# A two-block layer kernel on one core: gate steps as a pipeline, small products in one tile shape, other buffers and queues in the expert passes

## The chip, the cores and the metric

The kernel runs on one core of one Trainium2 chip. The metric is the device time of one execution in microseconds (us). A core has TensorE (PE, with its weight loads shown apart as PEld), VectorE (DVE), ScalarE (ACT), GpSimd (POOL) and SyncE (SP), and 16 DMA engines that serve the queues on which SP and ACT issue transfers.

## The reference

Two blocks are computed for 256 tokens of width 2048, all in fp32. The first has a recurrent time mix, an attention and an expert layer, the second a state-space scan and a windowed attention. The expert layer is the part on which most of the change bears: every token picks 16 of 16,384 experts in each of 8 heads, from the products of 128 by 128 keys.

```python
def step(S, inp):                       # recurrent mix, per head of 64
    r_t, k_t, v_t, kk_t, a_t, w_t = inp
    sa = jnp.einsum('bhvk,bhk->bhv', S, -kk_t)
    S = (S * w_t[:, :, None, :] + sa[..., None] * (kk_t * a_t)[:, :, None, :]
         + v_t[..., None] * k_t[:, :, None, :])
    return S, jnp.einsum('bhvk,bhk->bhv', S, r_t)
...
eid = jnp.take_along_axis(cand_id, pos, axis=-1)
gate = jax.nn.softmax(top_s, axis=-1).astype(h.dtype)
...
act = jax.nn.gelu(jnp.einsum('nd,nhkd->nhk', hx, expert_u[e]), approximate=False)
return jnp.einsum('nhk,nhkd->nd', gt * act, expert_v[e])
...
y_diag = jnp.einsum("bgcqs,bgrcqs,bcsgrp->bcqgrp", cb, decay_in, x_c)     # the scan
y_off = jnp.einsum("bcqgn,bcgrpn,bgrcq->bcqgrp", c_c, start_states, jnp.exp(da_cum))
return (y_diag + y_off).reshape(bsz, seqlen, nh, hp)
```

## The kernel before, in words

Large products run on PE as three: weights and tokens are split into a high part in the reduced fp32r form and a low rest, and hi times hi, hi times lo and lo times hi are added. `K.split` (L138 to L142) makes a split: ACT writes `hi`, then DVE or POOL subtracts it for `lo`. `K.wload` (L144) brings a weight tile of 1 MB from memory on SP's queue into one of two `raw` buffers. PE's line for a hi product has 512 columns, that for a lo product 256.

The stages, in us from the span's start: norm, the input product and the attention to 235; the recurrent mix, whose pairs of heads are woven with the input product, to 705; gates, output product and the expert query to about 1009; the first expert pass to 1862; the second to 2590; then the second block, with the scan groups inside 2650 to 3065.

**Pairs of heads** (`pair`, L442 to L688). Beside the split products they use small plain fp32 products, each of which is two records in the trace. `psA` (L464 to L467) has one of 64 rows of contraction, one of 128 and one of 32; `psS` (L547 to L558) 64 rows, head by head; `psQ` (L643) fills 64 of the 128 output columns of the array; `psY` (L659 to L666) mixes products of 64 and of 128 output columns. A row `64*128` in the trace gives rows and columns of such a tile.

**First expert pass** (`Peer.up`, L1159). All 16,384 experts are multiplied with all tokens, 128 of them (called "an expert" below) per step of the loop, with 1 MB of `peer_u`. The tile is turned on DVE (`tr`, L1172, four buffers), split in two halves c = 0 and c = 1 (L1176, `hi` and `lo` with three buffers each), and each half feeds eight hi and eight lo products (L1191, L1192). After both halves ACT copies a half of the sum (L239), DVE adds (L241), ACT applies the activation (L1200), and after every fourth expert ACT issues a store (L1202).

**Gates** (`Peer.gates`, L1118). The gate of every expert and token is the product of two one-hot factors. A step handles four tokens: DVE makes `oh2`, DVE or ACT the weighted `oh1` (two ACT instructions a token at L1145 and L1146), PE multiplies four 128 by 128 matrices into `psg` (L1151), and ACT copies `psg` to `scr` (L1132) in the next step. Every eighth step stores 2 MB to memory. There are 64 steps, 32 for each half of the tokens; the loop in `peer` (L1309 to L1317) spreads them over the first pass by a plan of rates (`UP_PLAN`, `G = 32`), one step per expert towards its end.

**Second expert pass** (`Peer.down`, L1219). For every eight experts (`B = 8`) ACT issues one load of 1 MB of activations and one of 1 MB of gates into two slots (L1240, L1241); DVE multiplies them (L1247), ACT and POOL split, and PE multiplies with `peer_v` (L1232 to L1234).

**Scan groups** (`Mamba.group`, L1465 to L1536). For two heads `psy` takes four products with 64 output columns (L1524) and two of full shape (L1526, L1529).

The order of instructions on each engine is set by a scheduler that simulates the program; buffers and an explicit tie (`issue_after`) bound it.

Of the kernel before, what the change touches and what calls it, by code (L numbers as in the profile page):

```python
# [9 lines left out]
F32 = mybir.dt.float32  # L10
F32R = mybir.dt.float32r
# [3 lines left out]
AF = mybir.ActivationFunctionType  # L15
ALU = mybir.AluOpType
# [4 lines left out]
T = 256  # L21
# [3 lines left out]
DMA_K = 2  # L25
# [85 lines left out]
class K:  # L111
# [32 lines left out]
    def wload(self, src, n=512):  # L144

        nc = self.nc
        raw = self.wp.tile([128, 4, 512], F32, tag="raw", bufs=RAW_BUFS, name="raw")
        if len(src.shape) == 3:
            for k in range(0, 4, DMA_K):
                nc.sync.dma_start(raw[:, k:k + DMA_K, :n], src[:, k:k + DMA_K])  # L150
        else:
            for c in range(4):
                nc.sync.dma_start(raw[32 * c:32 * c + 32, :, :n], src[c])
        return raw
# [219 lines left out]
class Rwkv:  # L374
# [56 lines left out]
    def lora(self):  # L431
        k, nc, pool = self.k, self.k.nc, self.pool
        th = self.th = pool.tile([65, T], F32, name="th")
        nc.vector.memset(th[64:65, :], 1.0)
        nc.scalar.activation(th[0:64, :], self.z[24][0:64, :], AF.Tanh)
        self.za = self.z[24]
        for z in (self.z[25], self.z[26][0:32]):
            k.sigmoid(z, z)

    WIDTH = 3  # L440

    def pair(self, hp):  # L442
# [15 lines left out]
        nc.scalar.dma_start(wg[:, 0, :], k.a["w_gate_up"][0, 0:128, fs])  # L458
        nc.scalar.dma_start(wg[0:32, 1, :], k.a["w_gate_up"][0, 128:160, fs])
# [87 lines left out]
        for h in range(2):  # L547
            ps = k.bank("psS").rearrange("p (a c b t) -> p a c b t", a=2, c=2, b=2)
            for tt in range(2):
                for cc in range(2):  # L550
                    E.matmul(ps[:, tt, cc], lhsT=two(BK[halves[h], tt, 2 * cc:2 * cc + 2]),
                             rhs=AR[halves[h], :, tt, halves[cc]], start=True, stop=True)
            for i, hs in enumerate(halves):
# [82 lines left out]
        for tt in range(2):  # L636
            starts = []
            for cc in range(2):
                cs = halves[cc]
                starts.append(Sd)  # L640
                if Sd is not None:
                    ps = k.bank("psQ")
                    E.matmul(ps[cs, 0:128], lhsT=At[:, tt, cs], rhs=Sd, start=True, stop=True)  # L643
# [15 lines left out]
            psY = k.bank("psY")  # L659
            for cc, s in enumerate(starts):  # L660
                cs = halves[cc]
# [326 lines left out]
class Peer:  # L988
# [129 lines left out]
    def gates(self, tt, scr, g_d, act):  # L1118
# [6 lines left out]
        late = None  # L1125
# [3 lines left out]
        def store(t0, ps):  # L1129
            c, t = divmod(t0, n)  # L1130
            st = scr[:, c % 2]
            S.copy(st.rearrange("p (i t) -> p i t", t=n)[:, :, t:t + 4], ps.rearrange("p (t i) -> p i t", t=4))  # L1132
            if t == n - 4:
                S.dma_start(g_d[c], st)

        for t0 in range(128 * tt, 128 * tt + 128, 4):
            ps = k.bank("psg")
            o2 = self.pool.tile([128, 4, 128], F32, tag="oh2", bufs=2, name="oh2")
            nc.vector.tensor_tensor(o2, key, tok(i2, t0), op=ALU.is_equal)
            o1 = self.pool.tile([128, 4, 128], F32, tag="oh1", bufs=2, name="oh1")  # L1140
            for j in range(4):
# [5 lines left out]
                else:  # L1147
                    nc.vector.tensor_scalar(o1[:, j], self.iota, i1[:, t:t + 1], w[:, t:t + 1], op0=ALU.is_equal,  # L1148
                                            op1=ALU.mult)
            for j in range(4):  # L1150
                nc.tensor.matmul(ps[:, j * 128:(j + 1) * 128], lhsT=o2[:, j], rhs=o1[:, j], start=True,  # L1151
                                             stop=True)
            if late:
                store(*late)
            late = (t0, ps)
            yield
        store(*late)

    def up(self, act_d):  # L1159
# [16 lines left out]
        def split(n, c):  # L1176
            hi, lo = (k.wp.tile([128, 8, 128], F32R, tag=n, bufs=HL_BUFS, name=n) for n in ("hi", "lo"))
# [41 lines left out]
    def down(self, scr, act_d, g_d, h, finish):  # L1219
# [6 lines left out]
        B = 8  # L1226
        held = []
# [7 lines left out]

        for i in range(128):
            raw = k.wload(V[i * 128:i * 128 + 128, :].rearrange("p (k f) -> p k f", k=4))
            if i % B == 0:
                x, g = (scr[:, 2 * (i // B % 2) + u, :].rearrange("p (i t) -> p i t", t=T) for u in range(2))
                nc.scalar.dma_start(x, act_d[:, i:i + B])  # L1240
                nc.scalar.dma_start(g.rearrange("p i t -> p (i t)").rearrange("p (c f) -> p c f", c=T // n),  # L1241
                                    g_d[:, :, i * n:(i + B) * n].rearrange("c p f -> p c f"))
                gv = g.rearrange("p i t -> p (i t)").rearrange("p (c i t) -> p c i t", c=T // n, i=B)
            if i % 2 == 0:
                xi = x[:, i % B:i % B + 2]
                xv = xi.rearrange("p i (c t) -> p c i t", t=n)
                nc.vector.tensor_tensor(xv, xv, gv[:, :, i % B:i % B + 2], op=ALU.mult)  # L1247
# [43 lines left out]
def peer(k, x2, xq, norm, hh, h_d, g_d, act_d, acts, es, finish):  # L1291
# [11 lines left out]
    with tc.tile_pool(name="up", bufs=1) as up:  # L1303
        pe.pool = up
        main = pe.up(act_d)
        route = [pe.route(up, tt) for tt in range(2)]
        gates = [pe.gates(tt, two, g_d, act) for tt, act in enumerate(GATE_ACT)]
        side = pe.anchored(itertools.chain(route[0], alternate(route[1], gates[0]), gates[1]))
        R, G, due = pe.ROUTE_STEPS, 32, 0.0  # L1309
# [61 lines left out]
class Mamba:  # L1371
# [93 lines left out]
    def group(self, g):  # L1465
# [36 lines left out]
        for hh in range(0, 8, 4):  # L1502
            M = []
            for ch in range(2):
# [12 lines left out]
                yield  # L1517
            for u in range(2):
                j = (hh + 2 * u) // 2
                hA = hh + 2 * u  # L1520
                ps = k.bank("psy")
                for ch in range(2):
                    for e in range(2):
                        E.matmul(ps[64 * e:64 * e + 64, ch * 128:(ch + 1) * 128], lhsT=xd[:, ch, hA + e, :],  # L1524
                                 rhs=M[ch][:, 2 * u + e, :], start=True, stop=True)
                E.matmul(ps[:, 256:384], lhsT=st[:, hA * 64:hA * 64 + 128], rhs=C[:, 128:256], start=True, stop=True)  # L1526
                db = W("db", [128, 2, 64])
                P.tensor_copy(db, self.dar[:, 1, h0 + hA:h0 + hA + 2, None].to_broadcast([128, 2, 64]))
                E.matmul(ps[:, 384:512], lhsT=db.rearrange("p e d -> p (e d)"), rhs=c["le"], start=True, stop=True)  # L1529
                ec = W("ec", [128, 128])  # L1530
                S.activation(ec, ps[:, 384:512], AF.Exp)
                V.tensor_tensor(ec, ps[:, 256:384], ec, op=ALU.mult)
                x = xs[j]
                V.scalar_tensor_tensor(x, x, self.dcol[:, 4 * g + j:4 * g + j + 1], ps[:, 0:T], op0=ALU.mult, op1=ALU.add)
# [525 lines left out]
```

## Time and profile before

| | |
|---|---|
| median of 3 runs | 3730.88 us (3727.95 to 3734.87) |
| the profiled execution's own time | 3734.22 us |
| its span | 3732.4 us |
| mean granted TensorE clock | 0.992 of full speed |
| busy over the span | PE 96%, PEld 80%, DVE 71%, ACT 53%, POOL 36% |
| mean DMA rate | 183 GB/s, 681.22 MB in all |

The profile is of one execution. PE's busy time is modelled: matmuls overlap, so the start of the next record is what tells how long one takes. A stage is read by the engines' busy time in its stretch, then by the waits there, each given with the instruction that ended it. In the view by stage a row gives the stretch, its length, then for PE, PEld, DVE, ACT and POOL the busy time with the number of instructions in brackets, the mean granted clock of PE as a share of full speed, the busy share of the DMA engines and GB/s.

### The profile page before, as it was taken

What the parts mean: (1) busy time and instruction counts of PE and PEld (TensorE: products, weight loads), DVE (VectorE), ACT (ScalarE), POOL (GpSimd) and SP (SyncE); (2) the same over time, 40 slices, a digit from 0 to 9 for tenths busy, and PEclk for the clock granted to TensorE, in tenths of its full rate; (3) what the DMA queues carried; (4) which work ended last, traced back from release to release, by engine and by line L of the source; (5) the groups of instructions that cost most, each with busy time, mean ns of one, the idle gap of its engine ahead of it and who ended that gap; (6) DMA issues with size and microseconds to landing.
All of it is one profiled execution on the core that took longest, in us unless ns stands there. A gap on an engine that the chain in (4) does not pass through costs nothing.

```text
span 3732.4 us, 56118 instructions
## 1 busy us (share of the span) xinstructions
PE 3596.9 (96%) x19815; PEld 2991.2 (80%) x19815; DVE 2663.3 (71%) x4261; ACT 1990.3 (53%) x3745; POOL 1329.2 (36%) x1328
## 2 busy tenths in 40 slices
PE   9999999999999999999899999999999999989998
PEld 7678888878888888877788888888788887878777
DVE  5766777667598898888644544446988879667776
ACT  5455555545454777666444444445555656445553
POOL 1333123221278777655511111111234444242101
PEclk9999999999999999999999999999999999999999
DMA  7443333467698888878877677665554445645444
GB/s 221 137 156 127 117 122 128 149 223 248 173 203 208 197 211 219 209 179 205 217 245 237 235 236 239 225 197 187 168 169 147 139 134 167 193 148 178 145 127 136
DMA packets 358334, 681.22 MB, mean 183 GB/s; under 512 B 43981, under 2 KB 111477, under 8 KB 354853
## 3 DMA queue, kind: packets, MB, share of 16 engines
q1 hardware_dynamic: 305216, 591.50, 54.3%
q10 hardware_dynamic: 52837, 86.14, 6.9%
q8 instruction: 157, 2.57, 0.3%
q14 instruction: 124, 1.02, 0.1%
HBM read 627.57 MB, written 47.22 MB: 181 GB/s over the span
## 4 chain that ended last, share of the span: by engine, by line
PE 45%; DVE 8%; issue 2%; ACT 1%; DMA 1%; POOL 0%; ACTq 0%; DVEq 0%; POOLq 0%
PE g L205 12%; PE g L207 6%; PE gv L1234 5%; PE gv L1233 5%; PE gv L1232 5%; DVE tr L1172 2%; DVE lo L142 2%; PE dv L1233 2%; PE dv L1232 2%; PE dv L1234 2%; DVE oh L1148 1%; ACT hi L140 1%; PE g L229 1%; PE g L230 1%; PE g L228 1%
## 5 line engine op out<-in xcount | busy, mean ns | idle before, releaser
L142 DVE TENSOR_TENSOR lo<-raw,hi 128x1024 fp32r<-128x1024 f32 (+3 forms) x856 | 1045.6, 1224 | 671.7 <-ACT hi L140 662.2
L140 ACT CAST hi<-raw 128x1024 fp32r<-128x1024 f32 (+3 forms) x858 | 868.2, 1015 | 957.5 <-PE g L205 336.4
L205 PE MATMUL g<-x,hi 128*128 128x512 f32 x3040 | 1089.0, 400 | 13.6 <-DVE x L1642 9.3
L207 PE MATMUL g<-x,lo 128*128 128x256 f32 x3040 | 843.5, 288 | 12.0 <-DVE lo L142 11.4
L1191 PE MATMUL gu<-x,hi 128*128 128x512 f32 x2048 | 734.1, 398 | 4.2 <-ACT hi L140 4.0
L142 POOL TENSOR_TENSOR lo<-tr,hi 128x512 fp32r<-128x512 f32 x429 | 593.0, 1411 | 265.7 <-ACT hi L140 184.6
L205 PEld LDWEIGHTS g<-x,hi 128*128 128x128 f32 x3040 | 567.5, 189 | 133.9 <-issue 18.3
L207 PEld LDWEIGHTS g<-x,lo 128*128 128x128 f32 x3040 | 574.0, 189 | 47.7 <-DVE lo L142 21.7
L1192 PE MATMUL gu<-x,lo 128*128 128x256 f32 x2048 | 581.7, 284 | 16.8 <-POOL lo L142 11.5
L1191 PEld LDWEIGHTS gu<-x,hi 128*128 128x128 f32 x2048 | 387.2, 189 | 91.9 <-ACT hi L140 6.0
L1192 PEld LDWEIGHTS gu<-x,lo 128*128 128x128 f32 x2048 | 388.0, 189 | 25.3 <-POOL lo L142 19.5
L1172 DVE STREAM_TRANSPOSE tr<-raw 128x1024 f32<-128x1024 f32 x256 | 309.4, 1232 | 87.1 <-POOL lo L142 47.1
L140 ACT CAST hi<-tr 128x512 fp32r<-128x512 f32 x512 | 289.9, 617 | 68.9 <-PE gu L1191 39.4
L142 POOL TENSOR_TENSOR g<-scr,g 128x512 fp32r<-128x512 f32 x64 | 112.3, 1756 | 574.3 <-ACT g L140 574.3
L1234 PE MATMUL gv<-hi,g 128*128 128x512 f32 x756 | 299.7, 396 | 0.0
L1233 PE MATMUL gv<-lo,g 128*128 128x512 f32 x756 | 299.7, 396 | 0.0
L1232 PE MATMUL gv<-hi,g 128*128 128x512 f32 x756 | 238.4, 396 | 0.0
L1200 ACT ACTIVATE act<-act 128x256 f32<-128x256 f32 x128 | 53.6, 419 | 239.3 <-DVE act L241 221.9
L205 PE MATMUL g<-y2m,hi 128*128 128x512 f32 x512 | 173.5, 395 | 0.0
L1233 PEld LDWEIGHTS gv<-lo,g 128*128 128x128 f32 x756 | 142.4, 188 | 34.7
L1234 PEld LDWEIGHTS gv<-hi,g 128*128 128x128 f32 x756 | 142.4, 188 | 34.7
L1232 PEld LDWEIGHTS gv<-hi,g 128*128 128x128 f32 x756 | 142.4, 188 | 34.7
(601 smaller groups left out, 5871.0 us busy)
## 6 DMA issues: line engine op xcount, KB each, us to landing
raw<-in_peer_u_dram SPq DMA_DIRECT2D x512, 256.0 KB
raw<-in_peer_v_dram SPq DMA_DIRECT2D x256, 512.0 KB
raw<-in_a_w_in_dram SPq DMA_DIRECT2D x160, 512.0 KB
raw<-in_w_in_dram SPq DMA_DIRECT2D x136, 512.0 KB
raw<-in_b_w_in_dram SPq DMA_DIRECT2D x64, 512.0 KB
raw<-in_a_w_out_dram SPq DMA_DIRECT2D x48, 512.0 KB
raw<-in_w_out_dram SPq DMA_DIRECT2D x32, 512.0 KB
raw<-in_w_peer_query_dram SPq DMA_DIRECT2D x32, 512.0 KB
```

The lines of the kernel that those rows point to most:

```text
L140: ins = nc.scalar.copy(hi, x) if heng == "act" else nc.vector.tensor_copy(hi, x)
L142: return ins, eng.tensor_tensor(lo, x, hi.bitcast(F32), op=ALU.subtract)
L205: nc.tensor.matmul(ps[f], lhsT=hi[:, k, f * 128:(f + 1) * 128], rhs=x2[:, q, :], start=(q == 0), stop=False)
L207: nc.tensor.matmul(ps[f][:, 0:T], lhsT=lo[:, k, f * 128:(f + 1) * 128], rhs=x2[:, q, 0:T], start=False, stop=(q == nk - 1))
L228: nc.tensor.matmul(ps[tt], lhsT=x, rhs=w, start=(q == 0), stop=False)
L1172: st["t"] = nc.vector.transpose(tr.rearrange("p b (u j) -> p u b j", u=2), raw[:, 2 * u:2 * u + 2].rearrange("p u (b j) -> p u b j", j=32))
L1191: nc.tensor.matmul(ps, lhsT=hi[:, j], rhs=self.hn2[:, q, :], start=(q == 0), stop=False)
L1192: st["m"] = nc.tensor.matmul(ps[:, 0:T], lhsT=lo[:, j], rhs=self.hn2[:, q, 0:T], start=False, stop=(q == KT - 1))
L1200: nc.scalar.activation(o, o, AF.Gelu)
L1232: nc.tensor.matmul(p, lhsT=x, rhs=hi, start=first, stop=False)
L1233: nc.tensor.matmul(p, lhsT=x, rhs=lo, start=False, stop=False)
L1234: nc.tensor.matmul(p, lhsT=g2[:, T + tt * 128:T + tt * 128 + 128], rhs=hi, start=False, stop=last)
```

## The change

1. *Gates.* A step now stores the product made one step ago, issues the product of the factors made one step ago, and makes factors for the next. The factors lie in a part of `hh` that is free then, three deep, not in tiles of their own. Each half has 34 steps for 32, and the plan's `G` is 34.
2. *First pass.* Halves c = 1 go to tiles of their own, `hi1` and `lo1` with two buffers, beside the three for c = 0.
3. *Second pass.* Loads are of 512 KB for four experts, on SP, in four slots; each is tied behind the weight fetch issued last, and the load of the next four experts is issued one expert into the present four.
4. *Small products.* `psA` and `psQ` use the full 128 by 128 shape over rows that are zero (memsets in `lora` and for `wg`); `psS` alternates between the two row halves; `psY` makes both heads at once and two copies take what is wanted; the scan's full-shape products come before the small ones of both units.

```diff
-                nc.sync.dma_start(raw[:, k:k + DMA_K, :n], src[:, k:k + DMA_K])
+                self.fetch = nc.sync.dma_start(raw[:, k:k + DMA_K, :n], src[:, k:k + DMA_K])
...
+        nc.gpsimd.memset(self.z[24][0:64], 0.0)
+        for r in (slice(32, 64), slice(64, 128)):
+            nc.gpsimd.memset(self.z[26][r], 0.0)
...
+        P.memset(wg[32:64, 1, :], 0.0)
...
-        E.matmul(psA[:, 0:T], lhsT=wg[64:128, 1, :], rhs=self.za[64:128, :], start=True, stop=True)
+        E.matmul(psA[:, 0:T], lhsT=wg[:, 1, :], rhs=self.z[24], start=True, stop=True)
         E.matmul(psA[:, T:], lhsT=wg[:, 0, :], rhs=self.z[25], start=True, stop=False)
-        E.matmul(psA[:, T:], lhsT=wg[0:32, 1, :], rhs=self.z[26][0:32, :], start=False, stop=True)
+        E.matmul(psA[:, T:], lhsT=wg[:, 1, :], rhs=self.z[26], start=False, stop=True)
...
+        for tt in range(2):
+            for cc in range(2):
+                for h in range(2):
+                    E.matmul(both[h][:, tt, cc], lhsT=two(BK[halves[h], tt, 2 * cc:2 * cc + 2]),
                              rhs=AR[halves[h], :, tt, halves[cc]], start=True, stop=True)
...
-                    E.matmul(ps[cs, 0:128], lhsT=At[:, tt, cs], rhs=Sd, start=True, stop=True)
+                    E.matmul(ps[:, 0:128], lhsT=At[:, tt], rhs=Sd, start=True, stop=True)
...
-                for h, hs in enumerate(halves):
-                    E.matmul(psY[hs, cs], lhsT=UV[:, tt, cc, h], rhs=MR[:, h, tt, cc], start=True, stop=(s is None))
+                E.matmul(psY[:, cc], lhsT=two(UV[:, tt, cc]), rhs=MR[:, :, tt, cc], start=True, stop=(s is None))
                 if s is not None:
-                    E.matmul(psY[:, cs], lhsT=s, rhs=Rh[:, tt, cs], start=False, stop=True)
-            S.copy(y[:, tt * 128:(tt + 1) * 128], psY[:, 0:128])
+                    E.matmul(psY[:, cc], lhsT=s, rhs=Rh[:, tt, None, halves[cc]].to_broadcast([128, 2, 64]), start=False,
+                             stop=True)
+            for h, hs in enumerate(halves):
+                S.copy(y[hs, tt * 128:(tt + 1) * 128].rearrange("p (c t) -> p c t", c=2), psY[hs, 0:2, h])
...
+        made, done = None, None
+        for t0 in range(128 * tt, 128 * tt + 136, 4):
+            if done:
+                store(*done)
+            done = product(*made) if made else None
+            made = factors(t0) if t0 < 128 * tt + 128 else None
             yield
...
-            hi, lo = (k.wp.tile([128, 8, 128], F32R, tag=n, bufs=HL_BUFS, name=n) for n in ("hi", "lo"))
+            if c == 0:
+                hi, lo = (k.wp.tile([128, 8, 128], F32R, tag=n, bufs=HL_BUFS, name=n) for n in ("hi", "lo"))
+            else:
+                hi, lo = (self.pool.tile([128, 8, 128], F32R, tag=n + "1", bufs=2, name=n) for n in ("hi", "lo"))
...
+        def load(b):
+
+            x, g = (scr[:, b % 4, u * 1024:u * 1024 + 1024] for u in range(2))
+            with k.tc.issue_after(k.fetch.ins):
+                nc.sync.dma_start(x.rearrange("p (i t) -> p i t", t=T), act_d[:, b * B:b * B + B])
+                nc.sync.dma_start(g.rearrange("p (c f) -> p c f", c=T // n), g_d[:, :, b * B * n:(b + 1) * B * n].rearrange("c p f -> p c f"))
...
-                nc.scalar.dma_start(x, act_d[:, i:i + B])
...
+            if i % B == 1 and i + B < 128:
+                load(i // B + 1)
...
+                E.matmul(ps[u][:, 256:384], lhsT=st[:, hA * 64:hA * 64 + 128], rhs=C[:, 128:256], start=True, stop=True)
+                E.matmul(ps[u][:, 384:512], lhsT=db.rearrange("p e d -> p (e d)"), rhs=c["le"], start=True, stop=True)
+            for u in range(2):
+                for ch in range(2):
+                    for e in range(2):
+                        E.matmul(ps[u][64 * e:64 * e + 64, ch * 128:(ch + 1) * 128], lhsT=xd[:, ch, hh + 2 * u + e, :],
+                                 rhs=M[ch][:, 2 * u + e, :], start=True, stop=True)
```

What the scheduler makes of it, at three places. First ACT near the end of the gate steps, before: `oh` is a factor (L1145, L1146), `scr<-psg` the copy of the product of the step before, `hi<-tr` a cast of a half's quarter, `half` and `act` the two ACT steps of an expert's sum.

```order
L1145 ACTIVATE oh_18697<-iota,pN_9359 128x128 x2
L1132 COPY scr<-psg 128x128x4
L1146 ACTIVATE oh_18697<-oh_18697,pI_9358,pN_9360 128x128 x2
L140 CAST hi<-tr 128x8x64 x2
L239 COPY half<-gu 128x256
L1200 ACTIVATE act<-act 128x256
```

And with the change:

```order
L1141 ACTIVATE hh<-iota,pN_9354 128x128 x2
L1142 ACTIVATE hh<-hh,pI_9353,pN_9355 128x128 x2
L140 CAST hi<-tr 128x8x64
L1214 ACTIVATE act<-act 128x256
L1157 COPY scr<-psg 128x128x4
L140 CAST hi<-tr 128x8x64 x3
L239 COPY half<-gu 128x256
```

The factors of a step now stand ahead of the copy of an earlier product and are not split by it; the casts stand in a run of three and one apart.

Second the loads for the second pass, where `scr<-act_d` and `scr<-g_d` are the activations and gates. Before they stand on ACT between the last experts' casts and activations:

```order
L1241 DMA scr<-g_d 128x8x256
L1240 DMA scr<-act_d 128x2048
L1241 DMA scr<-g_d 128x8x256
L1200 ACTIVATE act<-act 128x256
L140 CAST hi<-tr 128x8x64 x4
L239 COPY half<-gu 128x256
L140 CAST hi<-tr 128x8x64 x2
L1241 DMA scr<-g_d 128x8x256
L1200 ACTIVATE act<-act 128x256
```

With the change they stand on SP, between the fetches of both passes:

```order
L153 DMA raw<-in_peer_u_dram 32x4x512 x512
L1246 DMA scr<-act_d 128x1024
L1247 DMA scr<-g_d 128x8x128
L150 DMA raw<-in_peer_v_dram 128x1024 x4
L1246 DMA scr<-act_d 128x1024
L1247 DMA scr<-g_d 128x8x128
L150 DMA raw<-in_peer_v_dram 128x1024 x2
```

ACT has no load between its casts any more; the first pair of loads is ahead of the first `peer_v` fetch.

Third PE in a scan group, where L1524 is the small product and L1526 and L1529 are the full ones. Before:

```order
L205 MATMUL g<-x_78,hi 128x512
L1524 MATMUL psy<-m,xd 64x128 x2
L1526 MATMUL psy<-xs_25083,st 128x128
L1529 MATMUL psy<-const_ssd,db 128x128
L1524 MATMUL psy<-m,xd 64x128 x2
L1526 MATMUL psy<-xs_25083,st 128x128
L1529 MATMUL psy<-const_ssd,db 128x128
```

With the change:

```order
L1544 MATMUL psy<-xs_24982,st 128x128
L1545 MATMUL psy<-const_ssd,db 128x128
L1549 MATMUL psy<-m,xd 64x128 x4
L207 MATMUL g<-x_78,lo 128x256
```

The full-shape products stand in front, and small ones come in one run where there were two. Over the whole order the runs of L1524 go from 46 to 28, those of `psS` (L551, then L555) from 15 to 10; `psY` had 24 groups with small products and `psQ` 24 small products, and both have none now.

## Rows read from the trace of the kernel before

**Rows 1.** Busy time by stage (instructions in brackets), then clock, DMA share, GB/s
```profile
240.00:705.00 465.00, 450.68 (x2900) 376.03 (x2899) 332.29 (x645) 256.51 (x537) 133.87 (x224) 0.99 0.39 125
1009.00:1064.00 55.00, 50.69 (x286) 43.07 (x287) 42.19 (x135) 27.20 (x57) 42.55 (x35) 1.00 0.91 198
1064.00:1249.00 185.00, 181.79 (x1027) 156.71 (x1026) 154.43 (x271) 94.04 (x196) 151.72 (x114) 1.00 0.90 206
1249.00:1606.00 357.00, 348.38 (x2059) 304.73 (x2058) 312.74 (x506) 266.31 (x643) 264.58 (x191) 0.99 0.85 208
1606.00:1815.00 209.00, 188.39 (x1088) 158.85 (x1087) 173.92 (x190) 126.82 (x301) 115.61 (x82) 1.00 0.77 190
1815.00:1862.00 47.00, 36.90 (x176) 30.47 (x175) 23.63 (x28) 18.00 (x37) 25.26 (x19) 0.85 0.90 269
1862.00:2590.00 728.00, 727.30 (x3123) 585.13 (x3122) 358.46 (x326) 309.20 (x337) 110.64 (x66) 1.00 0.68 226
2650.00:3065.00 415.00, 415.00 (x2486) 347.20 (x2487) 354.82 (x645) 238.37 (x461) 167.28 (x229) 1.00 0.48 154
```

**Rows 2.** The same view, a stretch of the first pass without gate work
```profile
1064.00:1109.00 45.00, 44.66 (x255) 38.75 (x254) 42.07 (x101) 21.55 (x46) 36.32 (x29) 1.00 0.94 213
```

**Rows 3.** Groups on PE, 1606 to 1815: count, busy, mean of one, idle before
```profile
L1191 PE MATMUL gu<-x,hi 128*128 128x512 f32 x436 | 156.4, 399 | 0.0
...
L1151 PE MATMUL psg<-oh,oh 128*128 128x128 f32 x216 | 35.6, 300 | 20.6 <-ACT oh L1146 20.5
```

**Rows 4.** Timeline of PE: start, busy time, line, operation, form, count
```profile
119.31 6.47 PE L794 MATMUL psK<-csq,wuk 128*128 128x256 f32 x29
```

**Rows 5.** The waits in 1606 to 1815: us in total, times, longest
```profile
ACT act L1200 <- DVE act L241: 80.9, 28, 3.0
...
DVE lo L142 <- ACT hi L140: 31.8, 28, 1.6
...
PE psg L1151 <- ACT oh L1146: 20.5, 26, 1.2
```

**Rows 6.** Groups of instructions on PE, 1249 to 1606
```profile
L1192 PE MATMUL gu<-x,lo 128*128 128x256 f32 x879 | 251.0, 286 | 4.5 <-POOL lo L142 4.1
L1151 PE MATMUL psg<-oh,oh 128*128 128x128 f32 x296 | 47.2, 281 | 4.2 <-ACT oh L1146 3.9
```

**Rows 7.** Timeline of ACT, end of the first pass; idle before in brackets
```profile
1841.91 0.38 ACTq L1241 DMA_DIRECT2D scr<-g_d  x1
1842.33 0.42 ACT L1200 ACTIVATE act<-act 128x256 f32<-128x256 f32 x1 [11.36 <-DMA scr<-act_d]
```

**Rows 8.** Timeline of PE at the same place
```profile
1840.64 0.55 PE L1192 MATMUL gu<-x,lo 128*128 128x256 f32 x1 [4.70 <-DVE lo L142]
```

**Rows 9.** Timeline of PE among the pairs, psA
```profile
286.98 0.70 PE L465 MATMUL psA<-z,wg 64*128 64x256 f32 x2
...
288.86 0.71 PE L474 MATMUL psD<-wd,th 65*128 65x128 f32 x4
```

**Rows 10.** The same, psQ
```profile
339.95 0.39 PE L205 MATMUL g<-x,hi 128*128 128x512 f32 x1
340.27 0.43 PE L643 MATMUL psQ<-St,At 128*64 128x128 f32 x2
340.63 0.38 PE L207 MATMUL g<-x,lo 128*128 128x256 f32 x1
```

**Rows 11.** Timeline of PE among the scan groups, psy
```profile
2771.02 0.88 PE L1524 MATMUL psy<-m,xd 128*64 128x128 f32 x12
2771.83 0.49 PE L1526 MATMUL psy<-xs,st 128*128 128x128 f32 x2
2772.15 0.39 PE L1529 MATMUL psy<-const_ssd,db 128*128 128x128 f32 x2
2772.47 0.44 PE L1524 MATMUL psy<-m,xd 128*64 128x128 f32 x4
```

**Rows 12.** Timeline of ACT in the second pass
```profile
2108.39 1.05 ACT L140 CAST hi<-raw 128x1024 fp32r<-128x1024 f32 x1 [3.69 <-DMA raw<-in_peer_v_dram]
```

More of the change, by code (lines that the diff above doesn't have):

```diff
@@ L546, in pair @@
             P.memset(LK[hs, :, halves[i]], 0.0)
[L547 to L551, printed above, removed]
+        both = [k.bank("psS").rearrange("p (a c b t) -> p a c b t", a=2, c=2, b=2) for _ in range(2)]
+        for tt in range(2):
+            for cc in range(2):
+                for h in range(2):
+                    E.matmul(both[h][:, tt, cc], lhsT=two(BK[halves[h], tt, 2 * cc:2 * cc + 2]),
                              rhs=AR[halves[h], :, tt, halves[cc]], start=True, stop=True)
+        for h, ps in enumerate(both):
             for i, hs in enumerate(halves):
@@ L1124, in gates, with factors @@
         n = self.GATE_TOK
-        late = None
         tok = lambda x, t: x[:, t:t + 4, None].to_broadcast([128, 4, 128])
         key = self.iota[:, None, :].to_broadcast([128, 4, 128])
[L1129 to L1138, printed above, removed]
+        def factors(t0):
+            o2, o1 = (oh[:, t0 // 4 % 3, u].rearrange("p (j i) -> p j i", j=4) for u in range(2))
             nc.vector.tensor_tensor(o2, key, tok(i2, t0), op=ALU.is_equal)
-            o1 = self.pool.tile([128, 4, 128], F32, tag="oh1", bufs=2, name="oh1")
             for j in range(4):
@@ L1149, in gates, with product, store @@
                                             op1=ALU.mult)
+            return t0, o2, o1
+        def product(t0, o2, o1):
+            ps = k.bank("psg")
             for j in range(4):
[L1151 to L1155, printed above, removed]
+                nc.tensor.matmul(ps[:, j * 128:(j + 1) * 128], lhsT=o2[:, j], rhs=o1[:, j], start=True, stop=True)
+            return t0, ps
+        def store(t0, ps):
+            c, t = divmod(t0, n)
+            st = scr[:, c % 2]
+            S.copy(st.rearrange("p (i t) -> p i t", t=n)[:, :, t:t + 4], ps.rearrange("p (t i) -> p i t", t=4))
+            if t == n - 4:
+                S.dma_start(g_d[c], st)
+        made, done = None, None
[4 more added lines that the diff above has]
+            made = factors(t0) if t0 < 128 * tt + 128 else None
             yield
-        store(*late)
     def up(self, act_d):
@@ L1234, in mm @@
             nc.tensor.matmul(p, lhsT=g2[:, T + tt * 128:T + tt * 128 + 128], rhs=hi, start=False, stop=last)
+        load(0)
         for i in range(128):
@@ L1238, in down @@
             if i % B == 0:
[L1239 to L1243 removed]
+                x, g = loads.pop(i // B)
+            if i % B == 1 and i + B < 128:
+                load(i // B + 1)
             if i % 2 == 0:
@@ L1517, in group @@
                 yield
+            ps = [k.bank("psy") for _ in range(2)]
+            for u in range(2):
+                hA = hh + 2 * u
+                db = W("db", [128, 2, 64])
+                P.tensor_copy(db, self.dar[:, 1, h0 + hA:h0 + hA + 2, None].to_broadcast([128, 2, 64]))
+                E.matmul(ps[u][:, 256:384], lhsT=st[:, hA * 64:hA * 64 + 128], rhs=C[:, 128:256], start=True, stop=True)
+                E.matmul(ps[u][:, 384:512], lhsT=db.rearrange("p e d -> p (e d)"), rhs=c["le"], start=True, stop=True)
+            for u in range(2):
+                for ch in range(2):
+                    for e in range(2):
+                        E.matmul(ps[u][64 * e:64 * e + 64, ch * 128:(ch + 1) * 128], lhsT=xd[:, ch, hh + 2 * u + e, :],
+                                 rhs=M[ch][:, 2 * u + e, :], start=True, stop=True)
             for u in range(2):
                 j = (hh + 2 * u) // 2
[L1520 to L1529, printed above, removed]
                 ec = W("ec", [128, 128])
-                S.activation(ec, ps[:, 384:512], AF.Exp)
-                V.tensor_tensor(ec, ps[:, 256:384], ec, op=ALU.mult)
+                S.activation(ec, ps[u][:, 384:512], AF.Exp)
+                V.tensor_tensor(ec, ps[u][:, 256:384], ec, op=ALU.mult)
                 x = xs[j]
-                V.scalar_tensor_tensor(x, x, self.dcol[:, 4 * g + j:4 * g + j + 1], ps[:, 0:T], op0=ALU.mult, op1=ALU.add)
+                V.scalar_tensor_tensor(x, x, self.dcol[:, 4 * g + j:4 * g + j + 1], ps[u][:, 0:T], op0=ALU.mult, op1=ALU.add)
                 P.tensor_tensor(x[:, 128:256], x[:, 128:256], ec, op=ALU.add)
```

19 lines of the change are left out of this document (9 added, 10 removed).

## The prediction

> **What bounds the kernel now.** I read the busy times by stage first [rows 1]. PE is busy for 450.7 of 465 us among the recurrent pairs (240 to 705), 727.3 of 728 us in the second expert pass and all 415 us among the scan groups (2650 to 3065); no other engine comes near. There only less PE time helps. The first expert pass is different: PE is idle for 20.6 us in 1606 to 1815, 10.1 us in 1815 to 1862, where its granted clock is 0.85, and 8.6 us in 1249 to 1606. What ends those waits is therefore worth as much as PE's own work.
>
> The floor of the first pass comes from a stretch without gate work: 45 us hold 255 PE records, which is eight experts of 32 [rows 2], so 5.6 us for one expert and 0.35 us for one hi product with its lo product (by columns, 0.23 and 0.12). In 1606 to 1815 the hi products have 436 records [rows 3], 16 an expert, so there are 27.25 experts of 7.67 us each: 2.07 us over the floor. The 216 gate records are 27 steps of eight; at 0.11 us a record (half of a 256-column record, 6.47 us for 29 [rows 4]) a step is 0.9 us. So 6.50 us is PE's floor for an expert with its gate step, and 1.17 us of each period is wait.
>
> The waits say who holds it [rows 5]: PE's gate products wait 20.5 us in 26 waits for ACT's one-hot. ACT itself waits 80.9 us for DVE's sum before the activation, and DVE 31.8 us for ACT's hi. It is a circle: the factors, the product and the copy of one gate step lie one behind another within an expert's period, each on an engine that also splits weights.
>
> **The change, part by part.** The sum is made against the profiled execution (3734.2 us, 3.3 above the median of 3730.9).
>
> *Gate pipeline.* A step's factors are now made one step ahead, its product is issued a step later and its copy a step after that. Nothing is removed: the same one-hots, 64 products of four and 64 copies; two empty steps are added at each half's end, and 34 slots stand for 32 in the plan. What goes is PE's wait for ACT. Best case: PE's floor, 27.25 x (7.67 - 6.50) = -32. Worst: DVE is busy 173.9 us there, 6.38 us an expert [rows 1], and still waits 31.8 / 27.25 = 1.17 us an expert for ACT's hi [rows 5]; if that stays, the period is 7.55 and the gain 3. I take 6.75, a quarter of a microsecond over PE's floor, since the row of 20.5 us is the wait that PE itself sees and the five halves below shorten the other: 27.25 x 0.92 = **-25**.
>
> *Five halves in flight.* The c = 1 halves get two buffers of their own beside three for c = 0, so a hi may be written while earlier ones are still read. In 1249 to 1606 PE waits 4.5 us for a lo and 4.2 us for a gate factor [rows 6]; the stretch before, 1064 to 1249, is idle for 3.2 us [rows 1]. That is 12 us; I take **-10**. Bounds: -3 (POOL's own pace ends the waits for a lo) to -19: the 879 lo records are 55 experts and the 296 gate records 37 steps, 55 x 5.60 + 37 x 0.9 = 341 us of floor in 357, and the 3.2 before.
>
> *The start.* The second kind of half lives in a pool that opens after the query, so the first c = 1 split cannot start early as it did. PE is idle for 4.3 us of 1009 to 1064 [rows 1]. No row shows the new wait; between 0 and twice this idle time I take **+4**.
>
> *The end of the pass.* Here ACT issues the loads for the second pass in order. The load at 1841.91 has to wait for the slot that the first product frees; the activation behind it starts after 11.36 us of idle time [rows 7]. PE waits 4.70 us for a lo up to 1840.64 [rows 8], and the mean granted clock of 0.85 in this stretch [rows 1] says that some of it ran at the lower of the two levels (1.2 and 2.4 GHz). The 176 records of 1815 to 1862 [rows 1] are 5.5 experts, 30.8 us of floor in 47: 16 us of excess. The loads now go to SP, tied behind the weight fetches, four experts at a time with four slots, so ACT has no load in its order and neither activation nor hi waits behind one. I take 13 of the 16: **-13** (0 to -16; the last expert's chain from matmul to activation to store stays). What is moved: 32 loads of 1 MB leave ACT's queue; 64 of 512 KB join SP's. Behind each on SP stand the peer_v fetches; the first also stands ahead of the first fetch and waits for the last gate write. Fetches have their raw buffers to wait for, so I cost this at nothing, with PE's 727.3 of 728 us as cover; without the cover see the third rival.
>
> *Small products in one shape.* Around a small tile PE loses time at each change of shape. psA: six records take 1.88 us up to the next product [rows 9]; six of 0.22 are 1.32. So 0.56 a pair of heads, x 8 = 4.5, and entry 0.09 x 8 (from psQ) = 0.7: 5.2. psQ: from the hi before it to the lo after it is 0.68 us [rows 10]; a hi and two records of 0.11 are 0.45: 0.23 x 24 = 5.5. psy: 12 records of half the columns take 0.81 us, about six pairs of 0.11 running two at a time plus 0.15; then the full-shape pair takes 0.32 instead of 0.22, and so does the pair ahead of the next change [rows 11]. One excursion costs 0.35 us. The order of the instructions has 46 before and 28 now: 18 x 0.35 = 6.3. psS: 15 excursions become 10 (1.7). Its 64 products, eight for each pair of heads, are 128 records, 14.1 us at 0.11; they now alternate row halves, and if these run two at a time as psy's column halves do, 7 us go, if not none. I take 6. psY: 24 excursions at about 0.3 are 7; the merged products fill 128 columns where two halves ran side by side, which I price at 4: net 3. Together 27.7. In the pair stage 14.3 us of PE idle exist already, and a step that PE ends sooner can wait for DVE or ACT instead. I take **-25** (bounds: 0 to -32).
>
> The Trainium skill, "TensorEngine Tiling (Array Packing)", Key Properties, says that a change of tiling mode drains TensorE. The trace agrees with 0.23 to 0.35 us an excursion.
>
> *Added work.* Memsets of the low-rank tail and of wg run on POOL (133.9 of 465 us busy), psY's result takes two ACT copies for one: **+1** (0 to +3).
>
> **Sum:** -25 - 10 + 4 - 13 - 25 + 1 = -68 us, 3666 for the profiled execution, **3663** against the median. All good ends (-32, -19, 0, -16, -32, 0) make -99, so 3632; all poor ones (-3, -3, +8, 0, 0, +3) make +5.
>
> **Rivals.**
> 1. *DVE takes the wait's place* (0.14). For: 6.38 us busy and 1.17 us of waits for ACT's hi make 7.55, all but the present period; the five halves add no DVE or ACT throughput. Against: that wait is part of the circle, as ACT's is for DVE. The gate term falls to -3: 3663 + 22 = 3685.
> 2. *Shape is not the price* (0.12). A gap around psA or psQ may belong to the step from split products to plain fp32, which stays. Against: psy's full-shape pair, plain fp32 too, pays 0.10 after small ones [rows 11]. Then the 25 us go and unpacking psY costs its 4: 3663 + 29 = 3692. The Trainium skill, the same page, The Problem and The Solution, would split the array for contractions of 64 and less, with up to twofold speed; by that rule psA and psQ lose by being made full. The rows have their small products alone, with nothing beside them, so there the rule has nothing to speed up; I give this no more than the chance above.
> 3. *Slower: the loads on SP hold up the weight fetches* (0.05). In the second pass ACT's hi once waited 3.69 us for a peer_v transfer [rows 12] while PE, with 0.7 us of idle time in the whole pass [rows 1], went on. If each of the 32 pairs of loads exposes as much, 32 x 3.69 = 118: 3781. It decides from 68 / 32 = 2.1 us a pair. Against: DMA's share there is 0.68, and the bytes are the same.
> 4. *The buffers change nothing* (0.05): the transposed rows, not the halves, hold the splits back. The lo term falls to nothing: 3673, inside the main case.
>
> The forecast itself has 0.64.
>
> **Numbers.** A difference under 0.2%, 7.5 us, can't be told from none. Faster: the forecast, rivals 1, 2 and 4, less a little for two of them together, 0.93; within 0.2%: 0.02; slower: rival 3, 0.05. The range goes from the sum's good end, 3632, to past rivals 1 and 2, 3700; it leaves out rival 3 and the poorest sums.
>
> **What would show it.** Right: in the gate stretch the period near 6.75 us and no PE wait for the one-hot; at the pass's end no 11 us hole in ACT and a granted clock near 1; psA's six records in 1.3 us and fewer small-shape runs; the scan stage some 6 us shorter, the pair stage some 19. Wrong: a period above 7.4 with DVE busy; PE idle in the second pass with peer_v as the releaser; full-shape psQ still 0.68 us from hi to lo.

## The result and the profile after

The changed kernel takes 3713.41 us (median of 4 runs, 3708.23 to 3714.43) against 3732.88 us for the kernel before in the same rounds (3727.95 to 3737.76): ratio 0.9945, 95% interval 0.9928 to 0.9962. It is faster by 20 us where 68 were forecast, and outside the range of 3632 to 3700. The profiled execution took 3712.62 us with a span of 3710.8.

To see where the gain went, the program is cut at fixed points of the work: the first product of query and keys (at 943.3 us before, 935.5 after), the first hi product of every eighth expert (each sixteenth record of the first pass's hi line), the first product of the second pass and the first of the scan.

| stretch | before, us | after, us | difference | forecast |
|---|---|---|---|---|
| start to the query's keys | 943.3 | 935.5 | -7.8 | -19 |
| to expert 8 | 120.4 | 127.5 | +7.1 | +4 |
| experts 8 to 40 | 185.4 | 203.1 | +17.7 | -3 |
| experts 40 to 96 | 364.4 | 363.2 | -1.2 | -7 |
| experts 96 to 120 | 185.2 | 170.9 | -14.3 | -25 |
| expert 120 to the second pass | 63.2 | 51.0 | -12.2 | -13 |
| second pass to the first psy | 894.7 | 888.5 | -6.2 | 0 |
| rest of the span | 975.8 | 971.1 | -4.7 | -6 |

(The forecast is cut to the stretches by the prediction's own terms; its small products are 25, 6 of them in the scan, the gate term's 27 experts stand at the 24 of experts 96 to 120, and the +1 for added work is left out.) The busy times by stage, first of the kernel before at the cuts of experts 8, 40, 96 and 120, columns as in [rows 1]:

```profile
1063.70:1249.10 185.40, 182.19 (x1029) 157.07 (x1028) 154.83 (x272) 94.14 (x196) 152.12 (x114) 1.00 0.90 206
...
1613.50:1798.70 185.20, 166.49 (x963) 140.35 (x962) 155.53 (x170) 110.99 (x264) 102.36 (x72) 1.00 0.79 193
1798.70:1861.90 63.20, 51.27 (x260) 42.58 (x259) 35.61 (x42) 29.13 (x63) 34.12 (x25) 0.89 0.86 245
```

and of the changed kernel, the pair stage ahead of them:

```profile
240.00:698.00 458.00, 438.62 (x2847) 380.32 (x2845) 330.46 (x643) 262.58 (x551) 141.05 (x233) 0.99 0.41 130
1063.00:1266.10 203.10, 185.12 (x1029) 157.94 (x1028) 183.04 (x283) 98.17 (x200) 154.35 (x116) 0.99 0.84 191
...
1629.30:1800.20 170.90, 161.48 (x971) 140.93 (x970) 166.05 (x172) 114.65 (x271) 103.21 (x73) 0.99 0.82 204
1800.20:1851.20 51.00, 47.60 (x274) 40.87 (x273) 37.99 (x37) 27.96 (x59) 34.39 (x25) 1.00 0.87 248
```

The second row of the changed kernel is the surprise. PE has the same 1029 records there and 15 us more idle time, and DVE is busy 28 us longer. No instruction of DVE was changed there. The groups of instructions on DVE say which take longer; before, experts 8 to 40:

```profile
L1172 DVE STREAM_TRANSPOSE tr<-raw 128x1024 f32<-128x1024 f32 x65 | 79.0, 1232 | 27.7 <-POOL lo L142 23.7 <-DMA raw<-in_peer_u_dram 2.7 <-DVE lo L142 0.4
L142 DVE TENSOR_TENSOR lo<-tr,hi 128x512 fp32r<-128x512 f32 x16 | 20.8, 1303 | 1.0 <-ACT hi L140 1.0
...
L1095 DVE TENSOR_TENSOR oh<-oh,sif 128x256 f32<-128x256 f32 x16 | 10.7, 668 | 0.0
L1097 DVE TENSOR_REDUCE res<-oh 128x16 f32<-128x256 f32 x16 | 6.5, 407 | 0.0
L1093 DVE TENSOR_TENSOR oh<-abf,iota 128x256 f32<-128x256 f32 x16 | 6.2, 385 | 0.0
```

and after:

```profile
L1183 DVE STREAM_TRANSPOSE tr<-raw 128x1024 f32<-128x1024 f32 x64 | 78.2, 1233 | 11.9 <-POOL lo L142 9.4 <-DMA raw<-in_peer_u_dram 1.9
L142 DVE TENSOR_TENSOR lo<-tr,hi 128x512 fp32r<-128x512 f32 x16 | 25.3, 1583 | 0.2 <-ACT hi L140 0.2
L1101 DVE TENSOR_TENSOR oh<-oh,sif 128x256 f32<-128x256 f32 x16 | 19.4, 1211 | 0.0
L1099 DVE TENSOR_TENSOR oh<-abf,iota 128x256 f32<-128x256 f32 x16 | 19.0, 1185 | 0.0
...
L1103 DVE TENSOR_REDUCE res<-oh 128x16 f32<-128x256 f32 x16 | 6.5, 403 | 0.0
```

The same sixteen comparisons take 1185 ns each where they took 385, the products 1211 for 668, the lo halves 1583 for 1303; transposes and reductions are unchanged. A view of one moment, the timelines of POOL and then of DVE after the change, shows what they wait for:

```profile
1165.47 4.16 POOL L142 TENSOR_TENSOR lo<-tr,hi 128x512 fp32r<-128x512 f32 x3 [0.81 <-ACT hi L140]
```

```profile
1165.86 1.18 DVE L1099 TENSOR_TENSOR oh<-abf,iota 128x256 f32<-128x256 f32 x1
1166.97 0.41 DVE L1103 TENSOR_REDUCE res<-oh 128x16 f32<-128x256 f32 x1
1167.30 1.18 DVE L1101 TENSOR_TENSOR oh<-oh,sif 128x256 f32<-128x256 f32 x1
1168.40 1.77 DVE L142 TENSOR_TENSOR lo<-tr,hi 128x512 fp32r<-128x512 f32 x1
```

POOL's three instructions of 1.39 us end at about 1166.9, 1168.2 and 1169.6. DVE's three two-input instructions end soon after each, at 1167.04, 1168.48 and 1170.17; the reduction between them takes its usual 0.41. The view shows the delay as busy time of DVE, not as a wait.

The single records of the whole stretch show the same. After the change all 32 comparisons and products end 0.28 us after a POOL instruction that ran beside them, and 15 of the 16 lo halves 0.55 us after one. Before, no comparison does (14 of the 16 start as a POOL instruction ends, at most 0.07 us ahead of its end), nine of the products do (0.86 us each, the others 0.42) and nine of the lo halves (1.78, the others 0.67 to 0.73): a mean of 668 or 1303 ns mixes two durations.

The waits show how this reaches PE (1065 to 1240, before and then after):

```profile
ACT hi L140 <- PE gu L1191: 7.2, 16, 1.1
...
PE gu L1192 <- POOL lo L142: 3.1, 7, 1.1
```

```profile
ACT hi L140 <- DVE tr L1183: 60.0, 47, 3.7
POOL lo L142 <- ACT hi L140: 41.7, 29, 2.8
...
PE gu L1206 <- POOL lo L142: 12.3, 10, 1.8
```

Before, ACT's casts wait for a buffer that PE frees. After, they wait for DVE's next transpose, POOL for the cast, and PE for POOL's lo.

### The profile page after: what moved, and what is told of

The parts are those of the page before. It is cut to its first block, busy times and chain, and to the rows that moved or that the text cites. A ratio compares the mean times of both kernels' runs of the same rounds, so it can differ in the third digit from the quotient of the medians.

```text
span 3710.8 us, 55809 instructions
## 1 busy us (share of the span) xinstructions
PE 3570.0 (96%) x19751; PEld 2994.9 (81%) x19751; DVE 2739.3 (74%) x4261; ACT 2006.5 (54%) x3765; POOL 1335.0 (36%) x1339
## 4 chain that ended last, share of the span: by engine, by line
PE 44%; DVE 7%; DMA 2%; issue 2%; ACT 1%; SPq 0%; POOL 0%; DVEq 0%; ACTq 0%; POOLq 0%
PE g L205 12%; PE g L207 6%; PE gv L1254 5%; PE gv L1255 5%; PE gv L1253 5%; DVE lo L142 2%; PE dv L1255 2%; PE dv L1254 2%; PE dv L1253 2%; DVE tr L1183 1%; PE g L229 1%; PE g L230 1%; PE g L228 1%; DMA raw<-in_peer_u_dram 1%; ACT hi L140 1%
## 5 line engine op out<-in xcount | busy, mean ns | idle before, releaser
L142 DVE TENSOR_TENSOR lo<-raw,hi 128x1024 fp32r<-128x1024 f32 (+3 forms) x856 | 1068.0, 1251 | 616.7 <-ACT hi L140 606.8
L142 DVE TENSOR_TENSOR lo<-tr,hi 128x512 fp32r<-128x512 f32 x83 | 123.7, 1491 | 19.7 <-ACT hi L140 19.6
```

Of the source, the lines that this page charges most:

```text
L142: return ins, eng.tensor_tensor(lo, x, hi.bitcast(F32), op=ALU.subtract)
```

## The experiments

The theory of the loss: with five halves ACT casts ahead, POOL's lo instructions then lie beside DVE's two-input ones, which are held up by them, and DVE becomes the pace of experts 8 to 40.

**Five halves taken out of the change.**

```diff
-            if c == 0:
-                hi, lo = (k.wp.tile([128, 8, 128], F32R, tag=n, bufs=HL_BUFS, name=n) for n in ("hi", "lo"))
-            else:
-                hi, lo = (self.pool.tile([128, 8, 128], F32R, tag=n + "1", bufs=2, name=n) for n in ("hi", "lo"))
+            hi, lo = (k.wp.tile([128, 8, 128], F32R, tag=n, bufs=HL_BUFS, name=n) for n in ("hi", "lo"))
```

> The changed kernel with the c = 1 halves back in the three shared buffers; all else stays. Theory (port): with five halves ACT's casts run ahead, so GpSimd's lo casts fall on the same time as DVE's two-input instructions, which then take two to three times as long (0.39 to 1.18 us, 0.67 to 1.21 us, lo 1.30 to 1.58 us), and DVE paces the first 40 experts. Then the 25 us lost there come back: the first one-hot instructions of the route near 0.4 us again, experts 8 to 40 in 186 us instead of 203, and 3690 us (3685 to 3698). Rival 1 (only the late pool): the start alone comes back, some 8 us, 3705. Rival 2 (the loss is another part's, by the scheduler's order): 3713 within 5.

Measured: 3698.35 us, ratio to before 0.9893 (0.9876 to 0.9909), at the slow end of the expected range. Experts 8 to 40 take 184.1 us, and the comparison is back at 385 ns:

```profile
L142 DVE TENSOR_TENSOR lo<-tr,hi 128x512 fp32r<-128x512 f32 x16 | 20.8, 1303 | 1.0 <-ACT hi L140 1.0
...
L1101 DVE TENSOR_TENSOR oh<-oh,sif 128x256 f32<-128x256 f32 x16 | 10.7, 669 | 0.0
...
L1099 DVE TENSOR_TENSOR oh<-abf,iota 128x256 f32<-128x256 f32 x16 | 6.2, 385 | 0.0
```

Against the change this is 15 us, or 20 by the ratios. It is less than 25, since experts 96 to 120 go back to 183.1 us. The eight first experts (120.6 us) and experts 40 to 96 (355.0) get shorter as well, by 7 and 8 us. So five halves cost up to expert 96 and pay behind.

**Five halves alone** (the diff above the other way, on the kernel before, with the gates' factors in `hh`).

> The kernel before with five halves alone; the gates keep their old order, only their factors lie in the other buffer so that there is room. Theory (port): the first 40 experts lose some 25 us, and with the gate circle as before the time is 3733 + 15 to 25, about 3753. Rival 1 (only the late pool): 3733 + 8. Rival 2 (another part's loss): 3733 within 5, or faster by up to 10 if the waits for a lo shorten as the prediction had it.

Measured: 3745.37 us, ratio 1.003 (1.0019 to 1.0042): slower, but by 9 to 11 us, not by 20. Experts 8 to 40 take 203.8 us, and experts 96 to 120 172.0 us, without any gate pipeline. Experts 40 to 96 take 365.1 us. The theory had missed the gain behind them.

**Small products alone.**

> The kernel before with the small products alone. By start-to-start times of the changed kernel they save 17 us of PE time, and the pair stage gives 4 back as PE idle time: 3733 - 13, about 3720. Rival (the scheduler gave it back elsewhere): 3714 if the 19 us that the whole change gained are all theirs, 3733 if the order hides them.

Measured: 3713.04 us, ratio 0.9942 (0.9925 to 0.9958), 22 us: as much as the whole change gains, and the rival's 3714. The value is above the 13 expected, since the first pass was 9 us shorter too, mostly in a hole that moves from kernel to kernel (one expert near 91 takes 13.6 us before and 7.4 here). Why it does is not shown.

**Gate pipeline alone.**

> The kernel before with the gate pipeline alone, three shared halves. Theory: the pipeline breaks the wait of PE for ACT by itself; the last 24 gate experts go from 7.7 to about 7.0 us, and nothing changes before 1250: 3733 - 15, about 3718. Rival (it needs the five halves, since ACT's hi still waits for a buffer): 3730 or more.

Measured: 3728.53 us, ratio 0.998 (0.997 to 0.9989), 8 us. They lie in experts 40 to 96 (354.0 us for 364.4), where three other kernels with three halves and no pipeline take 356.1 to 361.2, so how much of it is the pipeline's is open. Experts 96 to 120 take 183.3 us, hardly less than 185.2. PE's groups there, before and then with the pipeline, say why:

```profile
L1192 PE MATMUL gu<-x,lo 128*128 128x256 f32 x385 | 107.6, 280 | 0.0
L1151 PE MATMUL psg<-oh,oh 128*128 128x128 f32 x192 | 31.7, 300 | 18.7 <-ACT oh L1146 18.7
```

```profile
L1197 PE MATMUL gu<-x,lo 128*128 128x256 f32 x385 | 110.7, 288 | 17.7 <-POOL lo L142 17.3
L1145 PE MATMUL psg<-hh 128*128 128x128 f32 x200 | 26.6, 276 | 0.5 <-ACT hh L1136 0.5
```

The pipeline does what it says: the wait for a factor is gone. A wait for POOL's lo of the same length stands in its place, which the kernels with five halves there do not have (the change waits 5.6 us for DVE's lo): the lo comes late by the three shared buffers. The forecast of 15 us is wrong, and the rival for this run, that it needs the five halves, is right for this stretch.

**Loads alone.**

> The kernel before with the loads of the second pass on SP alone (four experts a load, four slots). Theory: ACT's hole at the end of the first pass closes; the last experts and the change of pass, 63 us from expert 120 to the first product of the second pass, take about 52, and the second pass itself 2 to 3 us less: 3733 - 13, about 3720. Rival (the loads are not what holds the end; without five halves the wait for lo stays): 3730 or more. The prediction's third rival (fetches held up behind the loads): 3780.

Measured: 3730.09 us, ratio 0.9984 (0.9974 to 0.9994), 6 us. The difference lies between the two cases; the time alone looks like the rival's, but the kernel before took 3736 us in the same rounds. Expert 120 to the second pass takes 58.4 us (63.2 before) and the second pass, from its first product to its last, 2.5 us less. The third rival of the prediction does not occur.

**Five halves late**: shared buffers up to expert 90, where the gates come to one step an expert.

```diff
-            if c == 0:
+            if c == 0 or n < UP_FREE:
```

> The changed kernel with five halves only from expert 90 on; before that the three shared buffers. Theory: five halves cost in the first 90 experts and pay in the gate stretch behind them, where three halves left 7.6 us an expert. Then experts 96 to 120 go from 183 us to about 171, all else as with three halves: 3698 - 12, about 3686, faster than both kernels. Rival (GpSimd's casts hold DVE up there as well, so nothing is won): 3698 within 5.

Measured: 3679.08 us, ratio 0.9854 (0.9833 to 0.9875), 54 us faster than before and 34 faster than the change by the ratios. The comparison takes 477 ns on the mean in experts 8 to 40. Of the 34 us, 7 lie in the first eight experts, 18 in experts 8 to 40 and 8 in experts 40 to 96. Both halves of the finding are in its busy times (experts 8 to 40, then 96 to 120):

```profile
1052.20:1237.70 185.50, 182.45 (x1030) 157.09 (x1029) 155.33 (x272) 94.10 (x196) 150.97 (x114) 1.00 0.88 206
1592.50:1763.70 171.20, 161.99 (x971) 141.36 (x970) 165.95 (x172) 114.55 (x271) 103.19 (x73) 0.99 0.82 203
```

It came out 7 us under the expectation; some of that is ahead of the first pass, where single profiles of the same code lie 4.5 to 11.3 us under before.

**DVE and POOL by themselves.** Everything but a copy of the input to the output is left out.

> DVE and GpSimd instructions by themselves, everything else left out (the output is a copy of the input): on DVE eight each of a two-input comparison of 256 columns, a two-input subtraction of 512 columns, a reduction, a one-input scalar product and a max, and four transposes, first alone and then beside a chain of two-input subtractions on GpSimd. Theory (port): beside GpSimd the two-input instructions take up to the rest of a GpSimd instruction longer (0.4 to about 1.2 us, 0.7 to 1.5 or more), transposes, reductions and max the same as alone. Rival (memory contention of all kinds): all of them longer by a like share. Rival (no contention; the longer times have another source): none longer.

POOL's chain began at once, so that the first series was not alone as meant; the times alone come from the gap from 40.1 to 43.6 us in which POOL had nothing to do. The timeline of DVE, beside POOL up to 40.1 and from 43.6 on (`one`: one input, `two` and `lod`: two inputs):

```profile
31.81 1.23 DVE L2040 STREAM_TRANSPOSE turn<-xd 128x1024 f32<-128x1024 f32 x1
32.97 0.64 DVE L2038 TENSOR_TENSOR lod<-xd,hd 128x512 fp32r<-128x512 f32 x1
...
39.17 1.09 DVE L2044 TENSOR_SCALAR one<-xd 128x256 f32<-128x256 f32 x1
40.19 0.41 DVE L2042 TENSOR_REDUCE red<-xd 128x16 f32<-128x256 f32 x1
40.52 0.28 DVE L2044 TENSOR_SCALAR one<-xd 128x256 f32<-128x256 f32 x1
...
43.16 0.40 DVE L2047 TENSOR_TENSOR dend<-xd 128x256 f32<-128x256 f32 x1
...
52.27 1.14 DVE L2036 TENSOR_TENSOR two<-xd 128x256 f32<-128x256 f32 x1
53.33 1.74 DVE L2038 TENSOR_TENSOR lod<-xd,hd 128x512 fp32r<-128x512 f32 x1
55.00 1.48 DVE L2036 TENSOR_TENSOR two<-xd 128x256 f32<-128x256 f32 x1
```

A two-input instruction of 256 columns takes 0.40 us alone (one record) and 1.14 to 1.48 beside POOL (0.71 and 0.73 at the start of its chain), the one-input product 0.28 and 1.02 to 1.13. Reductions take 0.37 to 0.41 and max 0.41 in both, and transposes beside POOL the 1.23 that they take everywhere in the large kernels. So the delay is by kind of instruction, not general, as the theory had it, save that a one-input product is held up too. The two-input instructions that are held up end 0.28 us (256 columns) and 0.55 us (512) after a POOL instruction, as in the large kernel. Not every two-input instruction beside POOL is held: at 32.97, where it starts as a POOL instruction ends, the subtraction of 512 columns takes 0.64 for 1.74.

The Trainium skill, "SBUF — State Buffer", section "Who interferes with whom", says that DVE and GpSimd take a shared pair of ports in turn, for a whole instruction, when DVE's instruction has two inputs in SBUF or runs in a two-port mode, and that the order of issue decides who is held up. The trace agrees: the two-input instructions that were held up end 0.28 or 0.55 us after one of POOL's, and reductions are not held up.

**Late five halves with the old gate order.**

> The changed kernel with five halves only from expert 90 on and the gates in their old order (product in the same step as its factors, G of 32, factors in the moved buffer). Theory: the gate stretch is shortened by the five halves alone, so experts 96 to 120 stay at 172 us; the pipeline is worth 8 to 10 us in experts 40 to 96 (355 to 364 us): 3679 + 8, about 3687. Rival (the gate stretch needs the pipeline as well): back to 183 us there, 3679 + 12 + 8, about 3699.

Measured: 3687.00 us, ratio 0.9875 (0.9858 to 0.9891). Experts 96 to 120 take 170.6 us: the five halves alone shorten that stretch, and PE's wait for a factor there falls to 6.0 us without a pipeline. But experts 40 to 96 take 356.1 us against 354.8 with the pipeline, so the 8 us that were expected of it there are not seen either; the two kernels' intervals overlap. With the five halves late the pipeline's worth is not settled; by the medians it is 8 us.

**Five halves from expert 8 on.**

> The changed kernel with five halves from expert 8 on, shared buffers before. It parts the late pool from the port. Theory (port): the first eight experts take 55 us again instead of 62, experts 8 to 40 stay at 203 us with the one-hot comparison near 1.2 us: 3714 - 7, about 3707. Rival (the start put the engines out of step, and what follows is its wake): experts 8 to 40 at 185 us, about 3688.

Measured: 3711.10 us, ratio 0.9937 (0.9921 to 0.9954). From the first hi product to expert 8 it takes 54.5 us, 62.2 with the change; experts 8 to 40 take 206.9 us with the comparison at 1204 ns. The start and the ports are two separate costs, and the second is not the wake of the first.

**Late five halves with the old loads.**

> The changed kernel with five halves only from expert 90 on and the loads of the second pass back on ACT, eight experts a load. Theory: with five halves late the end of the pass is held by the loads as it was before; from expert 120 to the first product of the second pass 63 us instead of 52, the second pass 2 to 3 us more: 3679 + 13, about 3692. Rival (the five halves closed the hole by themselves): 3679 to 3684.

Measured: 3687.08 us, ratio 0.9866 (0.9849 to 0.9882). The end of the pass takes 55.0 us (51.9 with the new loads), not 63. Five halves close most of the hole by themselves; the loads are worth 3 us there, in a difference that the intervals do not tell apart.

## Why the prediction was wrong

Alone, by the ratios, the five halves make +11 us (forecast -10 and +4), the small products -22 (-25 and +1), the gates -8 (-25) and the loads -6 (-13). That is -24, near the -20 of the whole. So the five halves and the gates miss by some 17 us each, and the loads by 7.

- **Five halves, -10: the step that failed.** The prediction reasoned only with PE's waits and took more buffers to cost nothing beyond the start. By itself this part makes the kernel 0.3% slower. Its bound of +8 for the start holds (+7.1); what is missing is a price for DVE's instructions beside POOL's. The shorter wait of DVE for POOL's lo, 23.7 to 9.4 us, is more than paid for by its longer two-input instructions: 12.8 us for the comparisons, 8.7 for the products, 4.5 for the lo halves. Together that is 26 us of DVE's time, in a stretch that is 17.7 us longer. In experts 40 to 96, where -7 was forecast, five halves cost 8 us as well (363.2 us; 354.0 to 355.0 in the four kernels with the pipeline and three halves). That the instructions of one line changed their mean was there to be read before: [rows 1] has POOL busy 152 of 185 us in a stretch where DVE is too, and the lo on DVE takes 1303 ns beside POOL and 693 in the gate stretch of the same profile. I read the busy times as fixed.
- **Gate pipeline, -25: wrong cause.** PE's wait for a factor does vanish, as forecast from [rows 5], but by itself that wins 2 us in experts 96 to 120. Their period in the change is 7.1 us, not 6.75. What shortens them to 171 us is the five halves, with or without the pipeline. I took the wait that PE saw last for the cause; behind it a second one, for the lo, ended almost as late.
- **The first rival** (DVE takes the wait's place) was right in kind. In the first eight experts of that stretch the period is 7.1 us, and DVE is busy for 56.0 of 56.8 us:

```profile
1629.30:1686.10 56.80, 53.90 (x322) 46.30 (x321) 56.00 (x57) 37.68 (x89) 34.18 (x25) 1.00 0.83 204
```

  Its 7.55 was too much, since DVE's wait for ACT's hi did go; its busy time rose from 6.48 to 6.92 us an expert (155.53 and 166.05 by 24), with POOL beside it: the lo takes longer, the two-input one-hot shorter, the one-input product longer. Before, then after, experts 96 to 120:

```profile
L1148 DVE TENSOR_SCALAR oh<-iota,pI,pI 128x128 f32<-128x128 f32 x50 | 40.1, 840 | 0.0
L1139 DVE TENSOR_TENSOR oh<-iota,pI 128x512 f32<-128x512 f32 x24 | 38.4, 1602 | 0.0
L142 DVE TENSOR_TENSOR lo<-tr,hi 128x512 fp32r<-128x512 f32 x24 | 16.6, 693 | 27.3 <-ACT hi L140 27.3
```

```profile
L1144 DVE TENSOR_SCALAR hh<-iota,pI,pI 128x128 f32<-128x128 f32 x51 | 51.5, 1011 | 0.0
L142 DVE TENSOR_TENSOR lo<-tr,hi 128x512 fp32r<-128x512 f32 x24 | 38.7, 1613 | 0.9 <-ACT hi L140 0.9
L1136 DVE TENSOR_TENSOR hh<-iota,pI 128x512 f32<-128x512 f32 x25 | 19.2, 767 | 0.0
```

- **The end, -13: right in size** (-12.2, and a granted clock of 1.00 for 0.89), not in its cause alone: loads by themselves won 4.8 us, five halves by themselves 7.9 (63.2 to 55.3).
- **Small products, -25: right in kind, too large.** Alone they gave 22 us, but 9 of them in the first pass, where no small product was changed; in the stretches that hold them, up to the query's keys and from the second pass on, they gave 14. By start-to-start times of PE psS gained 4.5 us (7.7 forecast), psA 4.6 (5.2), psQ 2.9 (5.5), psY 1.0 (3), psy 6.1 (6.3). Up to the keys PE's busy time fell by 11.7 us in all, of which 3.9 came back as idle time; the cut from 27.7 to 25 had allowed for less. The row halves of psS do run two at a time, as assumed from psy, where they alternate as written: 16 records take 1.09 us to the next product, where 8 took 1.08 before. But that is so for two of the eight pairs of heads. In four the 16 take 1.20 to 1.62 us, and in two the scheduler left two runs of 8 with 1.08 each; hence 4.5 us and not 7.7.

```profile
361.71 1.16 PE L555 MATMUL psS<-AR,BK 64*128 64x128 f32 x16
362.80 0.39 PE L207 MATMUL g<-x,lo 128*128 128x256 f32 x1
```

  The same for psA, six records of 0.22 in 1.30 us where [rows 9] had 1.88:

```profile
245.72 0.59 PE L469 MATMUL psA<-z,wg 128*128 128x256 f32 x2
...
247.02 0.61 PE L478 MATMUL psD<-wd,th 65*128 65x128 f32 x4
```

  The second rival (shape is not the price) is refuted by these rows.
- **Rivals 3 and 4** did not occur: the second pass is not longer, and the buffers changed a great deal.
- The range left no room for a loss in a part that was thought to gain: its poor end for the five halves was -3. With +18 in place of -3 for experts 8 to 40 the sum would have been -47; the other two terms that came out 11 us short each, the gates and the pair stage, make up most of the rest.

What stays open: why POOL's and DVE's instructions start in the other order with five halves in experts 8 to 40, so that DVE's comparisons start beside a POOL instruction and not at its end. The runs show only that they do so in every kernel with five halves there (1185 to 1204 ns) and in none without (384 to 477).

## What to carry to other kernels

A buffer that lets one engine run ahead moves the work of the next ones in time as well, so ask which instructions will then lie beside each other, and price DVE's instructions at both durations that the trace shows, alone and beside POOL; the mean of a line can hide that there are two. When a wait is removed, look for the second one that ends just before it: here a wait for a factor gave way to one for a lo half of equal length. A resource that helps in one stretch and harms in another can be switched by stretch, and that was worth more than the whole change.

## What the runs showed of the hardware

A POOL instruction of 1.4 us beside them stretched DVE's two-input instructions of 256 columns from 0.40 to as much as 1.48 us, and a one-input product on DVE from 0.28 to about 1.09 us; transposes, reductions and max stayed as they were. A two-input instruction that starts as POOL's ends is not held up (0.64 us for 1.74 at 512 columns). The held two-input instructions end 0.28 us (256 columns) or 0.55 us (512) after the POOL instruction. The trace books this as busy time of DVE. On PE, products of 64 rows that alternate between the row halves start in pairs 7 ns apart, and 16 records take 1.09 us, as long as 8 do in a run of their own.
